# Attention's output halves added by a DMA within SBUF for three of four pairs of heads, and the epsilon term as a 65th column in the sum of the heads' squares

## The chip, the cores and the metric

The kernel runs on one core of a Trainium2 chip. The engines that matter are TensorE (PE, matrix products into PSUM), VectorE (DVE), ScalarE (ACT), GpSimd (POOL, which also issues DMAs on a queue of its own) and SyncE (SP, which only issues DMAs). Each engine takes its instructions in the order in which they are written into its queue. The metric is the device time of one execution in microseconds; runs of the kernel before gave a median of 1258.99 us.

## What is computed

One decoder layer on a sequence of 1024 tokens, width 1024. The part that matters here is attention: 8 heads of width 64, handled as four pairs, with an RMSNorm of each head of q and k, and stick-breaking weights in place of a softmax.

```python
def rms_norm(x, g):
    xf = x.astype(jnp.float32)
    y = xf * lax.rsqrt(jnp.mean(xf * xf, axis=-1, keepdims=True) + EPS)
    return (y * g.astype(jnp.float32)).astype(x.dtype)
...
    hn = rms_norm(h, norm1_g[i])
    proj = hn @ w_in[i]
    a_b, a_c, a_h, q, k, v, c_u, c_v = jnp.split(proj, split_idx, axis=-1)
    q = rms_norm(q.reshape(bsz, s_len, ATTN_HEADS, HEAD_DIM), q_norm_g[i])
    k = rms_norm(k.reshape(bsz, s_len, ATTN_HEADS, HEAD_DIM), k_norm_g[i])
    y_b = stick_breaking_attention(q, k, v).reshape(bsz, s_len, ATTN_W)
    h = h + jnp.concatenate([y_a, y_b, y_c], axis=-1) @ w_out[i]
...
        z = jnp.einsum('bqhd,bkhd->bhqk', qi, kj) * scale
        log_rem = jnp.where(causal, jax.nn.log_sigmoid(-z), 0.0)
        suffix = lax.cumsum(log_rem, axis=3, reverse=True) - log_rem
        weights = jnp.where(causal, jnp.exp(jax.nn.log_sigmoid(z) + suffix), 0.0)
        o = jnp.einsum('bhqk,bkhd->bqhd', weights, vj)
```

Convolution, spatial gating, the output projection, the squared-ReLU MLP and a gated input embedding complete the layer; the change does not touch them.

## The kernel before

Products are taken in three passes of parts: each float32 operand is split into a high part, rounded by ACT, and a low part, the difference, made by DVE or POOL (`split`).

`project(pr)` computes q, k and v of one pair of heads for eight blocks of 128 tokens. For each block PE accumulates a bank `qkv_ps` of 128x384. ACT squares the q and k columns into `qk_sq` (128 tokens by four head vectors of 64), DVE sums each 64 (L337), DVE scales the sums by 1/64 and adds an epsilon term that depends on the token (`ms1e[t]`, L339), POOL raises them to the power -1/2 (`rs`), and DVE multiplies q and k by that (`qk`, L345). `turn_qk` transposes the result on PE.

`attend(pr)` has eight steps, (head of the pair, group g of 256 query tokens). `stick` makes the weights: PE computes `z`, ACT two sigmoids (`rem`, `wt`), DVE a running product (the scan of L413), and DVE or POOL their product (L416). `gather` transposes the weights on PE (`w_tr`), splits them on ACT and DVE (`wT_hi`, `wT_lo`) and multiplies with V into `av`. V holds the high part of its 64 columns and the low part side by side, so rows 0 to 63 of `av` hold the one half of the output and rows 64 to 127 the other; they have to be added. That is L462 (ACT copies the lower rows to `av_lo`) and L463 (DVE adds them to the upper rows into `y_b`). `y_b` goes to `y_dram` by a DMA on SP, 128 rows for both heads of the pair, and is loaded again later for the output projection.

The order: `weave` interleaves attention of one pair with the projection of the next, or with the convolution for the last pair, by counts of matmul units. The tile framework then sets the order in each engine's queue by its own simulated timeline, and gives buffers out from pools (`half`, three buffers; `slot`, 56). On POOL's queue, `block_sums` sends transfers of 1 MB that build sums of blocks of a later weight matrix (`w_sums`) beside attention.

Of the kernel before, what the change touches and what calls it, by code (L numbers as in the profile page):

```python
# [7 lines left out]
F32 = mybir.dt.float32  # L8
F32R = mybir.dt.float32r
AF = mybir.ActivationFunctionType  # L10
ALU = mybir.AluOpType
AX = mybir.AxisListType

P = 128
# [4 lines left out]
HD = 64  # L19
# [13 lines left out]
def hybrid_block(ctx: ExitStack, tc: tile.TileContext, a: dict):  # L33
# [5 lines left out]
    nc = tc.nc  # L39
# [9 lines left out]
    tp = front.enter_context(tc.tile_pool(name="tp", bufs=6))  # L49
# [7 lines left out]
    def name(s):  # L57
        n_of[0] += 1
        return f"{s}_{n_of[0]}"

    def slot(s, dt=F32, shape=(P, HT)):
        return sp.tile(list(shape), dt, tag="slot", name=name(s))
# [10 lines left out]
    def halves(s, dt=F32, shape=(P, HT)):  # L73
        return [slot(s, dt, shape) for _ in range(2)]
# [1 line left out]
    def tmp(s, dt=F32, shape=(P, HT)):  # L76
        return tp.tile(list(shape), dt, tag="tmp", name=name(s))

    def half_tmp(s, dt=F32):
        return tp.tile([P, 256], dt, tag="half", name=name(s), bufs=3)  # L80

    def bank(pool, s):
        return pool.tile([P, HT], F32, tag=pool.name, name=name(s))
# [9 lines left out]
    half = [slice(0, HT), slice(HT, T)]  # L93
# [116 lines left out]
    ms1e, r1, r1h = [], [], []  # L210
# [89 lines left out]
                    nc.gpsimd.dma_start(w_sums[to, rows], src[rows])  # L300

    last_pool = [None]
    heads = {}
    y_dram = dram.tile([6, 2, P, HT], F32, name="y_dram")

    def project(pr):

        wk = [load_w(a["w_qkv"][pr, k], 384, nc.gpsimd if pr and k % 2 == 0 else nc.vector)
              for k in range(KT)]

        QS = [[None, None], [None, None]]

        KH = [[None, None], [None, None]]
        KL = [[None, None], [None, None]]
        V = [None] * 4
        low_q = [None, None]
        heads[pr] = QS, KH, KL, V, low_q
        for t in range(KT):
            th, ts = block(t)
            if t % 4 == 0:  # L320
                for hh, other in enumerate((hi_p, lo_p)):
                    KL[hh][th] = slot("KL", F32R)
                    nc.gpsimd.memset(KL[hh][th][other].bitcast(F32), 0.0)
                KH[0][th] = slot("KH", F32R)
                QS[0][th] = slot("QS", F32R)
                low_q[th] = slot("q_lo", F32R)
                QS[1][th] = slot("QS", F32R)
                KH[1][th] = slot("KH", F32R)
            ps = bank(ps_mm, "qkv_ps")[:, :384]
            for k0 in range(0, KT, 2):  # L330
                product(ps, [(cols(xn[k][th], ts), wk[k]) for k in (k0, k0 + 1)],
                        k0 == 0, k0 == KT - 2)
                yield 18
            sq = half_tmp("qk_sq")
            nc.scalar.activation(sq, ps[:, :256], AF.Square)
            ss = small.tile([P, 4], F32, tag="ss", name=name("ss"))
            nc.vector.tensor_reduce(out=ss, in_=sq.rearrange("p (h d) -> p h d", d=HD),  # L337
                                    axis=AX.X, op=ALU.add)
            nc.vector.tensor_scalar(out=ss, in0=ss, scalar1=1.0 / HD, scalar2=ms1e[t],  # L339
                                    op0=ALU.mult, op1=ALU.add)  # L340
            rs = small.tile([P, 4], F32, tag="rs", name=name("rs"))
            power_mhalf(rs, ss, 4)
            if t % 2 == 0:
                qk = tp.tile([P, 2, 256], F32, tag="qk", name=name("qk"), bufs=2)
            nc.vector.tensor_tensor(  # L345
                out=qk[:, t % 2].rearrange("p (h d) -> p h d", d=HD),
                in0=ps[:, :256].rearrange("p (h d) -> p h d", d=HD),
                in1=rs.unsqueeze(2).broadcast_to([P, 4, HD]), op=ALU.mult)
            if t % 2 == 0:
                V[t // 2] = slot("V", F32R, (P, 2, 2, 2, HD))  # L350
            v = V[t // 2][:, t % 2]
            split(ps[:, 256:].rearrange("p (h d) -> p h d", d=HD), v[:, :, 0], v[:, :, 1], scale=r1[t])
            if t % 2 == 1:
                later(72, lambda t=t, qk=qk: turn_qk(heads[pr], t, qk))
# [29 lines left out]
    def attend(pr):  # L384

        QS, KH, KL, V, _ = heads[pr]
        yb = halves("y_b")
        weights = {}

        def stick(hh, g):  # L390
            weights[hh, g] = []
# [31 lines left out]
        def gather(hh, g):  # L423
            own = slice(hh * HD, (hh + 1) * HD)
            wts = weights.pop((hh, g))
            av_of[0] ^= 1
            av = av_bank[:, av_of[0] * 256:(av_of[0] + 1) * 256]
# [17 lines left out]
            for j in range(-2, g + 1):  # L445
# [6 lines left out]
                for kb, o, first in parts:  # L452
                    m = 256 - first * P
                    lhs = V[kb // 2][:, kb % 2, hh].rearrange("p two d -> p (two d)")
                    for part in (hi, lo):
# [2 lines left out]
                                         stop=kb == 2 * g + 1 and part is lo)  # L458
                yield 8

            low = half_tmp("av_lo")
            nc.scalar.copy(low[:HD], av[HD:])  # L462
            nc.vector.tensor_tensor(out=yb[g // 2][own, (g % 2) * 256:(g % 2 + 1) * 256],  # L463
                                    in0=av[:HD], in1=low[:HD], op=ALU.add)
# [2 lines left out]

        steps = [(0, g) for g in range(4)] + [(1, g) for g in reversed(range(4))]
        yield from stick(*steps[0])
        for i, step in enumerate(steps):  # L470
            if i + 1 < len(steps):
                yield from stick(*steps[i + 1])
            block_sums(8 * pr + i, last_pool[0])
            yield from gather(*step)

    ATTEND = 2 * (72 + 8 * 10 + 72 + 10 * 10 + 80)

# [131 lines left out]
    for n in range(KT):  # L609
# [5 lines left out]
        for h in range(2):  # L615
            ps = wide_bank("pp_ps")
# [48 lines left out]
    ps = ctx.enter_context(tc.tile_pool(name="ps", bufs=8, space=PSUM, reuse_waits="tile"))  # L665
# [431 lines left out]
```

## Time and profile before

| | |
|---|---|
| median of 3 runs (lowest to highest) | 1258.99 us (1256.04 to 1264.21) |
| profiled execution | 1262.6 us |
| its span | 1260.9 us |
| PE busy in the span | 1215.0 us |
| DVE busy | 880.7 us |
| ACT busy | 603.8 us |
| POOL busy | 364.2 us |
| attention beside projections | 111 to 341 us of the span |

Times of lines and windows are microseconds from the start of the span; L12 is line 12 of the kernel. In the chain of waits each piece is followed back to what released it, so a piece of DVE in it is a moment at which all the rest waited for DVE. A busy PE is not PE at its peak, since matmuls are pipelined. The granted clock is the share of TensorE's full clock that was let through.

### The profile page before, as it was taken

What the parts mean: (1) busy time and instruction counts of PE and PEld (TensorE: products, weight loads), DVE (VectorE), ACT (ScalarE), POOL (GpSimd) and SP (SyncE); (2) the same over time, 40 slices, a digit from 0 to 9 for tenths busy, and PEclk for the clock granted to TensorE, in tenths of its full rate; (3) what the DMA queues carried; (4) which work ended last, traced back from release to release, by engine and by line L of the source; (5) the groups of instructions that cost most, each with busy time, mean ns of one, the idle gap of its engine ahead of it and who ended that gap; (6) DMA issues with size and microseconds to landing.
All of it is one profiled execution on the core that took longest, in us unless ns stands there. A gap on an engine that the chain in (4) does not pass through costs nothing.

```text
span 1260.9 us, 17509 instructions
## 1 busy us (share of the span) xinstructions
PE 1215.0 (96%) x5868; PEld 1034.1 (82%) x5868; DVE 880.7 (70%) x1324; ACT 603.8 (48%) x1167; POOL 364.2 (29%) x365
## 2 busy tenths in 40 slices
PE   9999898899999999879999999999999999999998
PEld 7898798898888878658888888888888888888887
DVE  7746886898979654676887777777755565686443
ACT  7725655666656454553334334344544344555211
POOL 2324434455323212233553453431000000122110
PEclk9999998999999999989999999999999999999999
DMA  9603257788542298689999999958956565653231
GB/s 309 211 18 117 84 158 210 167 210 159 119 114 38 67 292 226 175 221 251 269 244 255 252 244 250 252 193 302 354 179 224 183 223 170 203 166 106 76 111 51
DMA packets 118700, 234.89 MB, mean 186 GB/s; under 512 B 13105, under 2 KB 20529, under 8 KB 118353
## 3 DMA queue, kind: packets, MB, share of 16 engines
q1 hardware_dynamic: 94752, 168.08, 40.4%
q0 software_dynamic: 23856, 65.70, 23.3%
q8 instruction: 46, 0.75, 0.3%
q14 instruction: 46, 0.37, 0.1%
HBM read 176.57 MB, written 78.64 MB: 202 GB/s over the span
## 4 chain that ended last, share of the span: by engine, by line
PE 82%; DVE 8%; DMA 5%; issue 2%; ACT 1%; POOL 1%; SPq 0%; DVEq 0%; POOLq 0%; ACTq 0%
PE d_ps L731 24%; PE f_ps L731 24%; PE qkv_ps L161 3%; PE qkv_ps L162 3%; PE qkv_ps L163 3%; PE g_ps L161 2%; PE g_ps L163 2%; PE g_ps L162 2%; DVE rem L413 2%; PE av L456 2%; DMA S<-sq 2%; PE w_tr L438 1%; PE cv_ps L161 1%; DMA h_dram<-h 1%; PE cv_ps L162 1%
## 5 line engine op out<-in xcount | busy, mean ns | idle before, releaser
L135 DVE TENSOR_TENSOR w_lo<-raw,w_hi 128x512 fp32r<-128x512 f32 x268 | 244.9, 916 | 94.4 <-ACT w_hi L134 92.2
L134 ACT CAST w_hi<-raw 128x512 fp32r<-128x512 f32 x268 | 165.2, 619 | 242.6 <-PE d_ps L731 116.7
L731 PE MATMUL f_ps<-hn_hi,w_hi 128*128 128x512 f32 x448 | 176.5, 394 | 5.3 <-ACT v L884 5.3
L731 PE MATMUL f_ps<-hn_lo,w_hi 128*128 128x512 f32 x448 | 175.7, 392 | 0.0
L731 PE MATMUL f_ps<-hn_hi,w_lo 128*128 128x512 f32 x448 | 175.3, 392 | 0.0
L731 PE MATMUL d_ps<-f_hi,w_lo 128*128 128x512 f32 x448 | 174.3, 389 | 0.0
L731 PE MATMUL d_ps<-f_hi,w_hi 128*128 128x512 f32 x448 | 174.3, 389 | 0.0
L731 PE MATMUL d_ps<-f_lo,w_hi 128*128 128x512 f32 x448 | 174.3, 389 | 0.0
L731 PEld LDWEIGHTS f_ps<-hn_hi,w_hi 128*128 128x128 f32 x448 | 85.1, 190 | 23.4 <-ACT v L884 5.7
L719 POOL TENSOR_TENSOR S<-S,sq 128x512 f32<-128x512 f32 x14 | 22.6, 1614 | 273.5 <-ACT sq L788 273.5
L731 PEld LDWEIGHTS f_ps<-hn_lo,w_hi 128*128 128x128 f32 x448 | 85.1, 190 | 17.9 <-issue 0.2
L731 PEld LDWEIGHTS f_ps<-hn_hi,w_lo 128*128 128x128 f32 x448 | 85.0, 190 | 18.0
L731 PEld LDWEIGHTS d_ps<-f_hi,w_hi 128*128 128x128 f32 x448 | 84.1, 188 | 17.6
L731 PEld LDWEIGHTS d_ps<-f_lo,w_hi 128*128 128x128 f32 x448 | 84.1, 188 | 17.4
L731 PEld LDWEIGHTS d_ps<-f_hi,w_lo 128*128 128x128 f32 x448 | 84.1, 188 | 17.3
L413 DVE TENSOR_TENSOR_SCAN rem<-rem 128x128 f32<-128x128 f32 (+3 forms) x64 | 89.0, 1393 | 11.1 <-ACT rem L409 10.6
L161 PE MATMUL qkv_ps<-whi,xn_hi 128*128 128x384 f32 x256 | 92.0, 359 | 2.6 <-DVE V L138 2.6
L163 PE MATMUL qkv_ps<-whi,xn_lo 128*128 128x384 f32 x256 | 89.8, 351 | 0.0
L162 PE MATMUL qkv_ps<-wlo,xn_hi 128*128 128x384 f32 x256 | 89.8, 351 | 0.0
L135 DVE TENSOR_TENSOR f_lo<-raw,f_hi 128x512 fp32r<-128x512 f32 x112 | 77.6, 723 | 4.6 <-ACT f_hi L134 4.0
L134 ACT CAST f_hi<-raw 128x512 fp32r<-128x512 f32 x112 | 67.0, 620 | 17.9 <-DMA raw<-f_dram 13.4
L416 POOL TENSOR_TENSOR wt<-wt,rem 128x127 f32<-128x127 f32 (+4 forms) x40 | 44.3, 1109 | 107.7 <-DVE rem L413 44.9
(219 smaller groups left out, 2665.7 us busy)
## 6 DMA issues: line engine op xcount, KB each, us to landing
raw<-in_w_ff SPq DMA_DIRECT2D x160, 256.0 KB, 4.1
raw<-f_dram SPq DMA_DIRECT2D x112, 256.0 KB, 4.8
raw<-w_sums SPq DMA_DIRECT2D x64, 256.0 KB, 3.7
f_dram<-f SPq DMA_DIRECT2D x48, 256.0 KB, 4.4
f_dram<-t SPq DMA_DIRECT2D x48, 256.0 KB, 3.9
w_sums<-in_w_ff POOLq DMA_DIRECT2D x8, 1024.0 KB, 11.7
w_sums<-w_sums POOLq DMA_DIRECT2D x8, 1024.0 KB, 12.4
raw<-in_w_ff POOLq DMA_DIRECT2D x32, 256.0 KB, 5.4
```

The costliest lines, as they stand in the source:

```text
L134: nc.scalar.copy(hi, src)
L135: low.tensor_tensor(out=lo, in0=src, in1=hi, op=ALU.subtract)
L161: nc.tensor.matmul(ps, lh, rh, start=first and i == 0, stop=False)
L162: nc.tensor.matmul(ps, lh, rl, start=False, stop=False)
L163: nc.tensor.matmul(ps, ll, rh, start=False, stop=last and i == len(terms) - 1)
L413: nc.vector.tensor_tensor_scan(out=back, data0=back, data1=back, initial=1.0, op0=ALU.mult, op1=ALU.bypass)
L416: done = (nc.vector if on_vector else nc.gpsimd).tensor_tensor(out=wt[:, :W - 1], in0=wt[:, :W - 1], in1=rem[:, 1:W], op=ALU.mult)
L438: nc.tensor.transpose(tr[:, n:n + P], wts[i][:, kb * P:(kb + 1) * P], ident)
L456: nc.tensor.matmul(av[:, first * P:], lhs, part[:, o:o + m], start=kb == 0 and part is hi, stop=kb == 2 * g + 1 and part is lo)
L719: return eng.tensor_tensor(out=out, in0=x, in1=y, op=ALU.add)
L731: nc.tensor.matmul(bank, l, r, start=first and k == 0 and i == 0, stop=k == len(b) - 1 and i == 2, skip_group_check=True)
```

## The change

For the pairs 0, 1 and 2, ACT now copies all 128 rows of `av` into a tile `y_both` of 128x512, two groups into one tile. When both are there, a DMA on POOL's queue adds rows 64 to 127 onto rows 0 to 63 within SBUF. The store of the 64 rows is put off: it is called after the next even step, or in the next pair's attention after its first `stick`. The DVE addition is gone for these pairs; pair 3 keeps `y_b`. In the projection, `qk_sq` gets 65 columns for each head: ACT writes the epsilon term into the 65th, scales the squares by 1/64 as it makes them, and the reduction of L337 sums 65 columns, so that L339 is gone for all 32 blocks.

```diff
-    def half_tmp(s, dt=F32):
-        return tp.tile([P, 256], dt, tag="half", name=name(s), bufs=3)
+    def half_tmp(s, shape=(P, 256)):
+        return tp.tile(list(shape), F32, tag="half", name=name(s), bufs=3)
...
     last_pool = [None]
+    later_stores = []
...
-            sq = half_tmp("qk_sq")
-            nc.scalar.activation(sq, ps[:, :256], AF.Square)
+
+            sq = half_tmp("qk_sq", (P, 4, HD + 1))
+            nc.scalar.copy(sq[:, :, HD], ms1e[t].broadcast_to([P, 4]))
+            nc.scalar.activation(sq[:, :, :HD], ps[:, :256].rearrange("p (h d) -> p h d", d=HD),
+                                 AF.Square, scale=HD ** -0.5)
             ss = small.tile([P, 4], F32, tag="ss", name=name("ss"))
-            nc.vector.tensor_reduce(out=ss, in_=sq.rearrange("p (h d) -> p h d", d=HD),
-                                    axis=AX.X, op=ALU.add)
-            nc.vector.tensor_scalar(out=ss, in0=ss, scalar1=1.0 / HD, scalar2=ms1e[t],
-                                    op0=ALU.mult, op1=ALU.add)
+            nc.vector.tensor_reduce(out=ss, in_=sq, axis=AX.X, op=ALU.add)
...
-        yb = halves("y_b")
-        weights = {}
+        yb = halves("y_b") if pr == 3 else None
+        weights, both, summed, seen_g = {}, [None], [], []
+
+        def store_rows():
+
+            while summed:
+                to, t = summed.pop(0)
+                nc.sync.dma_start(to, t[:HD])
...
+            if yb is None:
+                if both[0] is None:
+                    both[0] = slot("y_both")
+                t = both[0]
+                nc.scalar.copy(t[:, (g % 2) * 256:(g % 2 + 1) * 256], av)
+                if len(seen_g) % 2:
+                    nc.gpsimd.dma_start(t[:HD], t[HD:], accum_op=ALU.add)
+                    summed.append((y_dram[pr, g // 2, own], t))
+                    both[0] = None
+                seen_g.append(g)
+                return
             low = half_tmp("av_lo")
...
         yield from stick(*steps[0])
+        while later_stores:
+            later_stores.pop(0)()
         for i, step in enumerate(steps):
...
             yield from gather(*step)
+            if i % 2 == 0:
+                store_rows()
+        later_stores.append(store_rows)
```

The framework orders the queues anew. Three places show what moved; the lines of the changed kernel are its own (L338 the square, L337 the column, L341 the reduction, L472 the av copy, L474 the addition by DMA).

ACT before, in pair 0 beside the projection of pair 1: sigmoids of `z` and squares of two blocks.

```order
L335 ACTIVATE qk_sq_1597<-qkv_ps_1512 128x256
L409 ACTIVATE rem_1485<-z_1487 128x128
L410 ACTIVATE wt_1486<-z_1487 128x128
L409 ACTIVATE rem_1485<-z_1493 128x512
L410 ACTIVATE wt_1486<-z_1493 128x512
L137 ACTIVATE V_1509<-qkv_ps_1512,r_566 128x2x64
L409 ACTIVATE rem_1519<-z_1521 128x256
L410 ACTIVATE wt_1520<-z_1521 128x256
L335 ACTIVATE qk_sq_1695<-qkv_ps_1607 128x256
L409 ACTIVATE rem_1519<-z_1527 128x512
```

ACT now, at the square of the same second block and the one after it.

```order
L416 ACTIVATE rem_1516<-z_1524 128x512
L417 ACTIVATE wt_1517<-z_1524 128x512
L338 ACTIVATE qk_sq_1691<-qkv_ps_1603 128x4x64
L337 COPY qk_sq_1994<-ms_726 128x4
L416 ACTIVATE rem_1578<-z_1580 128x384
L417 ACTIVATE wt_1579<-z_1580 128x384
L416 ACTIVATE rem_1578<-z_1586 128x512
L417 ACTIVATE wt_1579<-z_1586 128x512
L338 ACTIVATE qk_sq_1788<-qkv_ps_1703 128x4x64
L134 CAST wT_hi_1636<-w_tr_1631 128x512
L134 CAST wT_hi_1651<-w_tr_1646 128x512
L337 COPY qk_sq_2102<-ms_726 128x4
```

The column of a block three further on is written right behind a square (`qk_sq_1994` behind `qk_sq_1691`): the pool has three buffers, and 1994 takes that of 1691, so this copy waits for DVE's reduction of 1691.

DVE before, in pair 0 beside the projection of pair 1: the addition into `y_b`, the reductions and the scaling of their sums.

```order
L463 TENSOR_TENSOR y_b_1345<-av_87,av_lo_1854 64x256
L379 COPY QS_1409<-q_lo_1410 64x512
L337 TENSOR_REDUCE ss_1922<-qk_sq_1920 128x4
L135 TENSOR_TENSOR wT_lo_1945<-w_tr_1939,wT_hi_1944 128x512
L135 TENSOR_TENSOR wT_lo_1960<-w_tr_1954,wT_hi_1959 128x512
L339 TENSOR_SCALAR ss_1922<-ss_1922,ms_726 128x4
L337 TENSOR_REDUCE ss_2001<-qk_sq_1999 128x4
L413 SCALAR_TENSOR_TENSOR rem_2019<-rem_2019 128x384
L413 SCALAR_TENSOR_TENSOR rem_2029<-rem_2029 128x512
L339 TENSOR_SCALAR ss_2001<-ss_2001,ms_726 128x4
L345 TENSOR_TENSOR qk_1927<-qkv_ps_1811,rs_1925 128x256
```

DVE now, at the same place (scan of 384 and of 512 columns).

```order
L423 TENSOR_TENSOR wt_1874<-wt_1874,rem_1873 128x767
L135 TENSOR_TENSOR wT_lo_1940<-w_tr_1934,wT_hi_1939 128x512
L135 TENSOR_TENSOR wT_lo_1955<-w_tr_1949,wT_hi_1954 128x512
L341 TENSOR_REDUCE ss_1997<-qk_sq_1994 128x4
L420 SCALAR_TENSOR_TENSOR rem_2014<-rem_2014 128x384
L420 SCALAR_TENSOR_TENSOR rem_2024<-rem_2024 128x512
L135 TENSOR_TENSOR wT_lo_1973<-w_tr_1968,wT_hi_1972 128x384
L346 TENSOR_TENSOR qk_1922<-qkv_ps_1927,rs_1999 128x256
```

The addition and both scalings are gone; the reduction stands alone, and POOL's `rs` follows it at once.

POOL before, at the first steps of pair 1: weight products, the 1 MB transfers and `rs`.

```order
L416 TENSOR_TENSOR wt_2339<-wt_2339,rem_2338 128x383
L300 DMA w_sums<-in_w_ff 16x16384 x2
L169 TENSOR_TENSOR rs_2379<-ss_2376,mhalf 128x4
L169 TENSOR_TENSOR rs_2476<-ss_2473,mhalf 128x4
L416 TENSOR_TENSOR wt_2401<-wt_2401,rem_2400 128x639
L300 DMA w_sums<-in_w_ff 16x16384 x2
L169 TENSOR_TENSOR rs_2586<-ss_2583,mhalf 128x4
```

POOL now, at the same place.

```order
L423 TENSOR_TENSOR wt_2329<-wt_2329,rem_2328 128x383
L300 DMA w_sums<-in_w_ff 16x16384 x2
L474 DMA y_both_2188<-y_both_2188 64x512
L169 TENSOR_TENSOR rs_2369<-ss_2367,mhalf 128x4
L169 TENSOR_TENSOR rs_2465<-ss_2463,mhalf 128x4
L423 TENSOR_TENSOR wt_2390<-wt_2390,rem_2389 128x639
L300 DMA w_sums<-in_w_ff 16x16384 x2
L474 DMA y_both_2387<-y_both_2387 64x512
L169 TENSOR_TENSOR rs_2574<-ss_2572,mhalf 128x4
```

Two additions stand right behind pairs of 1 MB transfers on the same queue, and ahead of `rs`.

## The prediction

> **What bounds the kernel now.** I read the page's first two parts, then the busy time by stage, then the chain that ended last in the stage that the change edits, and last the timelines of single engines there. The profiled execution took 1262.6 us, of which 1260.9 is the span. The table of stages has the columns us, PE, PEld, DVE, ACT, POOL (each busy us and instructions), granted PE clock, DMA share and GB/s.
>
> ```profile
> core 0: us, PE busy (x) PEld busy (x) DVE busy (x) ACT busy (x) POOL busy (x), PEclk, DMA share, GB/s
> 57.00:111.00 54.00, 53.90 (x309) 50.41 (x308) 26.26 (x77) 18.80 (x43) 15.28 (x18) 1.00 0.06 23
> 111.00:170.00 59.00, 51.67 (x307) 48.37 (x306) 47.58 (x73) 36.12 (x85) 26.64 (x25) 0.94 0.33 116
> 170.00:230.00 60.00, 54.53 (x327) 51.91 (x325) 44.28 (x82) 35.06 (x85) 27.70 (x31) 0.91 0.65 194
> 230.00:290.00 60.00, 53.78 (x340) 50.59 (x340) 54.82 (x93) 38.16 (x94) 31.91 (x32) 0.97 0.89 205
> 290.00:341.00 51.00, 46.60 (x309) 43.98 (x308) 45.63 (x75) 35.19 (x83) 19.38 (x18) 1.00 0.64 120
> 560.00:860.00 300.00, 300.00 (x1318) 247.94 (x1318) 231.14 (x267) 117.65 (x201) 129.62 (x118) 1.00 0.90 248
> ```
>
> From 560 us on, PE is full, so what is won earlier reaches the end. From 57 to 111 PE is full as well (53.90 of 54): the first pair's projection, which runs there, gains nothing from less DVE work. Attention beside the next pair's projection, 111 to 341 us, is different: PE is busy 206.6 of 230 us and idles 23.4, and DVE is busy 192.3. The chain says who is late there.
>
> ```profile
> by line: PE qkv_ps L161 11.7%; DVE rem L413 11.2%; PE qkv_ps L162 10.9%; PE qkv_ps L163 10.8%; PE av L456 6.2%; issue 5.3%; DVE wT_lo L135 4.6%; PE w_tr L438 4.2%; DMA stage<-in_w_qkv 3.7%; DVE ss L339 2.8%; DVE wt L416 2.5%; DVE KL L370 2.
> 131.15 0.43 DVE y_b L463
> 155.28 1.03 DVE ss L339
> 176.68 0.77 DVE ss L339
> 189.96 8.72 DMA stage<-in_w_qkv
> ...
> 272.26 1.98 DVE ss L339
> 317.80 0.32 DVE y_b L463
> ```
>
> This is the window 111 to 346 us. Scans (L413) are the largest DVE share and stay. Two operations that the change takes off DVE are in the chain themselves: L339 with 2.8% of 235 us, 6.6 us, and L463 with twelve pieces, the first and last shown, that add up to 4.4 us.
>
> **The change, part by part.** First the operations in that window, by form, and why L339 costs what it does.
>
> ```profile
> L339 DVE TENSOR_SCALAR ss<-ss,ms 128x4 f32<-128x4 f32 x26 | 11.0, 427 | 0.3
> L463 DVE TENSOR_TENSOR y_b<-av,av_lo 64x256 f32<-64x256 f32 x22 | 9.0, 411 | 1.5 <-ACT av_lo L462 1.2
> L339 DVE TENSOR_SCALAR ss<-ss,ms x32: 203/229/1984, 82.3 to 345.6; 128x4 f32<-128x4 f32 x32
> L337 DVE TENSOR_REDUCE ss<-qk_sq x32: 399/419/421, 81.9 to 343.7; 128x4 f32<-128x256 f32 x32
> 152.02 0.40 DVE L337 TENSOR_REDUCE ss<-qk_sq 128x4 f32<-128x256 f32 x1
> ...
> 272.26 1.98 DVE L339 TENSOR_SCALAR ss<-ss,ms 128x4 f32<-128x4 f32 x1
> 272.24 1.97 POOL L135 TENSOR_TENSOR wlo<-stage,whi 128x384 fp32r<-128x384 f32 x2
> ```
>
> L339 has four columns and a median of 229 ns, but up to 1984 ns. The last two rows, of the engines' timelines, show why: the long one started 0.02 us after POOL's wlo products and ended 0.03 us after them (272.24 + 1.97 = 274.21 against 274.24). It waited for POOL in its own slot. The reduction L337 never does (399 to 421 ns). So 26 L339 take 11.0 us of DVE in the window, about 5 of them standing. They go; the reduction gets 260 columns for 256, four columns more of 419 ns: nothing that counts.
>
> Of the 32 L463 the 24 of the first three pairs go, 22 of them by this window's count. DVE loses 20.0 (11.0 + 9.0) of its 192 us. On the chain that is 6.6 + 4.4 = 11.0 us. Not all of it arrives: the load of 8.72 us at 189.96 is followed by ACT and PE, and its landing is not set by DVE. I take what lies ahead of it as swallowed there: L463 at 131, 151 and 171 us (0.43 + 0.41 + 0.43) and L339 at 155 and 176 us (1.03 + 0.77), 3.1 us. That leaves 7.9. If the load moves forward with the rest, it is 11.0; if scans take every place freed, it is 0.
>
> What is added lands on ACT, POOL, SP and the DMA queues.
>
> ```profile
> L335 ACT ACTIVATE qk_sq<-qkv_ps 128x256 f32<-128x256 f32 x26 | 9.9, 384 | 6.2 <-PE qkv_ps L163 5.8
> L462 ACT COPY av_lo<-av 64x256 f32<-64x256 f32 x22 | 8.1, 370 | 6.8 <-PE av L456 6.4
> L410 ACT ACTIVATE wt<-z 128x128 f32<-128x128 f32 x11 | 3.2, 292 | 6.4 <-PE w_tr L438 6.4
> L790 POOL DMA_DIRECT2D S<-sq x14 | 12.0, 860 | 19.7 <-ACT sq L788 9.8 <-DMA S<-sq 8.2 <-DMA raw<-in_xT 0.7
> L300 POOL DMA_DIRECT2D w_sums<-in_w_ff x16 | 8.7, 547 | 0.0
> L297 POOL DMA_DIRECT2D w_sums<-w_sums x7 | 8.1, 1438 | 0.1
> ```
>
> ACT, av: a copy of 128x256 takes the place of one of 64x256. L335 reads 128x256 in 384 ns, L462 370: 14 ns each, 0.3 us for 24, which hides like the next. PE's next av group then waits for ACT alone and no longer for DVE behind it.
>
> ACT, the column: 26 copies of 128x4 in the window. No row has it; the nearest, 128x128, takes 292 ns, which is the upper end; the lower is 0, where it fits in an idle gap. I take 0.25 us, 6.5 us of ACT. ACT is busy 144.5 of the 230 us, so this alone hides.
>
> ACT, the wait: this is the part with teeth. The column copy of tile n+3 writes the buffer whose reduction on DVE has to be over, and the order puts it right behind the square of tile n: of 29 such copies 13 have none or one ACT row in between, five of them before attention, where ACT is idle most of the time (18.80 of 54 us busy), and eight in the window. ACT stands there until DVE has reduced, and behind it stand the w_tr and z evictions that feed DVE and PE. How late is the reduction? A short and a long case:
>
> ```profile
> 126.61 0.38 ACT L335 ACTIVATE qk_sq<-qkv_ps 128x256 f32<-128x256 f32 x1 [0.72 <-PE qkv_ps L163]
> 127.03 0.42 DVE L337 TENSOR_REDUCE ss<-qk_sq 128x4 f32<-128x256 f32 x1 [2.04 <-ACT qk_sq L335]
> 253.27 0.39 ACT L335 ACTIVATE qk_sq<-qkv_ps 128x256 f32<-128x256 f32 x1
> 256.14 0.41 DVE L337 TENSOR_REDUCE ss<-qk_sq 128x4 f32<-128x256 f32 x1
> ```
>
> From the end of the square to the end of the reduction 0.46 and 2.89 us; the mean over 16 pairs that I could match in the timelines is 1.07. Eight copies standing 1.07 less 0.25 of work in between make 6.6 us of ACT; the others, with two to six rows between, wait only on long backlogs like the second case, and I put them at 3.4 in all: 10 us. Since ACT idles more than a third of the window and part of this falls into its gaps, I charge a quarter, 2.5 us. The ends are 0 and 27.8 us (26 copies, 1.07 each, all on the path).
>
> POOL: twelve DMA issues. Nearest in kind is L790, an addition by DMA into SBUF, 860 ns; the ends are 547 (L300) and 1438 (L297). Twelve make 10.3 us (6.6 to 17.3) on an engine busy 105.6 of 230 us. Each also waits for ACT's av copy, with rs and wt products queued behind it. POOL is in the chain for only a few pieces, so I charge 0.5 us.
>
> SP: twelve stores replace six, each 0.33 us of issue, on a queue that mostly waits: 0. They wait for the additions to land; behind them stand w_qkv and w_conv loads, and slots of y_both are reused by memsets on POOL and copies on ACT. That is a rival, below.
>
> Clock: rows of 6 us where DVE is full and PE short.
>
> ```profile
> 154.00:160.00 6.00, 3.91 (x15) 3.67 (x16) 5.90 (x9) 1.75 (x5) 2.77 (x2) 0.72 0.00 0
> 232.00:238.00 6.00, 3.25 (x19) 2.50 (x20) 5.92 (x10) 4.30 (x10) 2.81 (x3) 1.00 1.13 208
> 238.00:244.00 6.00, 6.00 (x30) 6.00 (x29) 4.81 (x5) 0.40 (x2) 2.98 (x1) 0.72 1.13 208
> ```
>
> A PE gap is followed by a granted clock of 0.72, which costs 0.28 x 6 = 1.7 us. The clock of the three stages from 111 to 290 us (0.94, 0.91, 0.97) holds 0.06 x 59 + 0.09 x 60 + 0.03 x 60 = 10.7 us of this. I count one such slice as saved, 1.7, because the gap before the first row holds a long L339.
>
> Sum: -7.9 + 2.5 + 0.5 - 1.7 = -6.6 us, 1256.0 against the profiled 1262.6. That execution lies 3.6 above the median of the three runs shown (1258.99), so the forecast is 1252.4, given as 1252.
>
> **The rivals.** *A, more is won.* All 11.0 us arrive and five slices at 0.72 go (8.5 us): 19.5, so 1239.5 on the median's scale. For it: qk waits for the rs that waits for L339, and the 3.9 us from the end of the reduction at 152.42 to that of its L339 at 156.31 shrink to nothing. Against: scans stay and fill DVE. The Trainium skill (TensorE: Matmul & The Clock Gate, What's actually happening) states that the clock falls after an idle window of about 3.4 us. By that rule these shorter gaps would cost no clock, and A would give 11.0 us only, 1248; the trace's 0.72 rows disagree, and I keep the row.
>
> *B, slower: ACT stands behind DVE.* If three quarters of the 27.8 us reach the path, 20.9 less 7.9 makes 13.0 us more, 1272; all of it makes 1279. Three quarters is the point from which it decides. For it: DVE has backlogs of 2 to 3 us, in which the reduction waits behind scans. Against: ACT's slack, 85 us.
>
> *C, the additions land late and give the gain back.*
>
> ```profile
> w_sums<-w_sums POOLq DMA_DIRECT2D x7, 1024.0 KB, 14.4
> y_dram<-y_b SPq DMA_DIRECT2D x5, 256.0 KB, 8.0
> ```
>
> Five of the twelve additions stand right behind a pair of 1 MB transfers on the same queue. At 14.4 us to land, and 8.0 for the store, a slot comes free 22 us after the issue; a step of attention takes about 230/24 = 9.6. At the places where a memset or an av copy wants that slot, an engine stops; two such stops of 3 to 4 us give 1259. The Trainium skill (SBUF — State Buffer, Door 1 and its section on the setup cost) says that 64 partitions reach 8 of the 16 ports, 196 GB/s measured. By that alone the 128 KB land in some 2.7 us, an estimate from that page with its 2 us fixed cost, and C would be void; I hold with the queue's row.
>
> *D, nothing arrives*: scans fill every freed place, 1259.
>
> **How the numbers follow.** Forecast 0.45 (1247 to 1258), A 0.20, C 0.15, D 0.10, B 0.10. The likeliest gives 1252. The range 1240 to 1268 takes in most of A and half of B's 27.8 us (13.9 - 7.9 = 6.0, 1265), with POOL at its upper end (17.3 us) for the rest; outside stay the rest of B and a little of A. A change of under 1%, 12.6 us, is about what a measurement of this kernel can tell from none: faster 0.20 (A), slower 0.10 (B), within 0.70.
>
> **What would show it.** DVE in the attention stage down by some 20 us, no TENSOR_SCALAR beside the reduction, and y_b in the last pair alone; PE idle below 23 us. Right for the ACT term: waits of ACT's 128x4 copy on the reduction add to 10 us or less. Wrong: those waits add to 20 or more with w_tr evictions late; or POOL memsets and y_both copies wait for the stores; or the DVE time falls and PE's idle time does not. A change after 443 us, where the order only shifts by a few rows, would be outside this account.

## The result and the profile after

The changed kernel takes 1240.82 us (median of four runs, 1238.52 to 1243.24) against 1261.42 us of the kernel before, measured beside it: a ratio of 0.9846, with an interval of 0.9821 to 0.9871. It is 1.3 to 1.8% faster, where the forecast was 1252. The profiled execution has a span of 1241.5 us, 19.4 less than before. Of all runs behind the ratios below one was slow, 1713.93 us for the column with L339's work aside, and no ratio counts it.

Two stages, the projections of the pairs with attention beside them (from the first to the last `qkv_ps` product) and the output projection (`o_ps`), hold most of it. Columns as in the table of stages above; first the changed kernel, then the one before.

```profile
75.10:324.10 249.00, 236.67 (x1479) 226.49 (x1478) 195.51 (x313) 159.96 (x406) 120.81 (x126) 0.97 0.63 158
426.60:522.10 95.50, 94.03 (x406) 76.42 (x406) 55.16 (x88) 52.91 (x92) 23.01 (x31) 0.98 0.85 244
```

```profile
76.20:339.60 263.40, 239.88 (x1479) 227.69 (x1478) 208.34 (x365) 157.19 (x374) 115.95 (x116) 0.96 0.56 143
443.40:543.10 99.70, 96.34 (x405) 77.00 (x406) 53.87 (x86) 51.64 (x90) 24.04 (x32) 0.97 0.82 226
```

The first stage is 14.4 us shorter: TensorE idles 12.3 us for 23.5, which is 11.2, and the same 1479 recorded products take 3.2 us less. About half of that is the clock: it was granted at one half for 20.5 us of the stage before and for 17.1 us now, and half of the difference is 1.7 us. The output projection is 4.2 shorter. The stretch ahead of the first stage gives 1.1, the convolution's end 1.3, the tail 0.4; the next 320 us give 2.0 back, and the last two large stages do not change.

What TensorE waited for in the first stage (us, times, the longest), changed kernel first:

```profile
PE w_tr L445 <- DVE KL L371: 3.8, 3, 1.7
PE w_tr L445 <- DVE wt L423: 2.5, 3, 1.4
PE av L463 <- DVE wT_lo L135: 2.0, 4, 0.8
...
PE z L409 <- ACT wt L417: 1.4, 5, 0.4
PE av L463 <- ACT y_both L472: 0.5, 2, 0.3
```

```profile
PE qk_tr L364 <- DVE qk L345: 5.6, 4, 2.7
PE av L456 <- DVE wT_lo L135: 4.0, 4, 1.7
...
PE av L456 <- DVE y_b L463: 2.6, 4, 1.3
PE w_tr L438 <- DVE wT_lo L135: 2.2, 1, 2.2
```

The largest wait of before, for `qk`, is gone altogether; that for y_b became 0.5 us for ScalarE's copy; those for `wT_lo` fell as well, and 1.4 us for `wt` came in. The largest single part of it is time lost on the way of a block of q and k from its product to `qk` and the transposition. That way has its steps on four engines: product (TensorE), square (ScalarE), reduction and, before the change, L339 (VectorE), rs (POOL), qk (VectorE). It is what the experiments below turn on, so here it is from the trace of each kernel. Each block has eight L163 products; the first column is the time from the end of the eighth to the start of the block's square, the second from the square's end to the end of the block's `qk` (means over the 26 or 27 blocks whose square starts after 105 us).

```
kernel                     product to square   square to qk   first qkv_ps to first o_ps
before                           2.02 us          5.89 us            367.2 us
before, second execution         2.04             5.98               368.3
changed                          0.49             4.40               351.6
changed, second execution        0.50             4.46               350.5
```

The second part lost L339's step. The first lost 1.5 us a block, although the change does nothing at that place. One block of the kernel before shows how: its product ended at 199.37 + 0.34 = 199.71, and ScalarE squared it at 204.28. Timelines of ScalarE, VectorE and POOL (start, us, what):

```profile
203.89 0.37 ACT L462 COPY av_lo<-av 64x256 f32<-64x256 f32 x1
204.28 0.38 ACT L335 ACTIVATE qk_sq<-qkv_ps 128x256 f32<-128x256 f32 x1
```

```profile
205.89 0.42 DVE L463 TENSOR_TENSOR y_b<-av,av_lo 64x256 f32<-64x256 f32 x1
206.34 0.42 DVE L337 TENSOR_REDUCE ss<-qk_sq 128x4 f32<-128x256 f32 x1
206.67 0.48 DVE L138 SCALAR_TENSOR_TENSOR q_lo<-qk_tr,c_gq,QS 128x256 fp32r<-128x256 f32 x1
207.07 0.22 DVE L339 TENSOR_SCALAR ss<-ss,ms 128x4 f32<-128x4 f32 x1
```

```profile
207.37 1.04 POOL L169 TENSOR_TENSOR rs<-ss,mhalf 128x4 f32<-128x4 f32 x1 [2.84 <-DVE ss L339]
```

The square stands directly behind an `av_lo` copy, and its reduction behind that copy's y_b addition. Squares and `av_lo` come from one pool of three buffers, `half`, and the framework sets the order with it. In the order of the kernel before, 15 of the 32 squares stand directly behind an `av_lo` copy; in the changed one, whose first three pairs take no `av_lo`, 3 of 32 stand directly behind an `av_lo` or `y_both` copy. No wait in the trace of the kernel before is put down to that pool, so if it costs time, it does so through the order.

### The profile page after: what moved, and what is told of

The parts are those of the page before. It is cut to its first block, busy times and chain, and to the rows that moved or that the text cites. A ratio compares the mean times of both kernels' runs of the same rounds, so it can differ in the third digit from the quotient of the medians.

```text
span 1241.5 us, 17505 instructions
## 1 busy us (share of the span) xinstructions
PE 1207.3 (97%) x5868; PEld 1029.7 (83%) x5868; DVE 871.1 (70%) x1268; ACT 604.5 (49%) x1199; POOL 369.0 (30%) x377
## 4 chain that ended last, share of the span: by engine, by line
PE 83%; DVE 6%; DMA 5%; issue 3%; ACT 2%; POOL 1%; SPq 0%; POOLq 0%; ACTq 0%; DVEq 0%
PE d_ps L754 25%; PE f_ps L754 24%; PE qkv_ps L161 3%; PE qkv_ps L162 2%; PE qkv_ps L163 2%; PE g_ps L161 2%; PE g_ps L163 2%; PE g_ps L162 2%; DVE rem L420 2%; PE av L463 2%; DMA y_both<-y_both 2%; PE w_tr L445 2%; PE o_ps L161 2%; PE o_ps L163 2%; PE o_ps L162 2%
## 5 line engine op out<-in xcount | busy, mean ns | idle before, releaser
L420 DVE TENSOR_TENSOR_SCAN rem<-rem 128x128 f32<-128x128 f32 (+3 forms) x64 | 92.2, 1446 | 18.7 <-ACT rem L416 17.6
L163 PE MATMUL qkv_ps<-whi,xn_lo 128*128 128x384 f32 x256 | 89.1, 348 | 0.0
L423 POOL TENSOR_TENSOR wt<-wt,rem 128x127 f32<-128x127 f32 (+4 forms) x40 | 47.1, 1194 | 82.5 <-DVE rem L420 39.9
```

The source lines that it names most:

```text
L163: nc.tensor.matmul(ps, ll, rh, start=False, stop=last and i == len(terms) - 1)
L420: nc.vector.tensor_tensor_scan(out=back, data0=back, data1=back, initial=1.0, op0=ALU.mult, op1=ALU.bypass)
L423: done = (nc.vector if on_vector else nc.gpsimd).tensor_tensor(out=wt[:, :W - 1], in0=wt[:, :W - 1], in1=rem[:, 1:W], op=ALU.mult)
```

## The experiments

Eighteen runs were made, two of them of the unaltered kernels, each in five rounds with the kernel before on the same chip. Ratios are to it; 0.01 is 12.6 us. Three theories stand at the start. W: VectorE's work is what is won, as the prediction reckoned. Q: the way from the reduction to `qk`, which L339 lengthened (as P, with the square at its start, it comes back below). O: any shift of the framework's order would win.

**One part alone.** The column without the addition by DMA, the addition without the column, and L339 as an activation of ScalarE:

```diff
-            nc.vector.tensor_scalar(out=ss, in0=ss, scalar1=1.0 / HD, scalar2=ms1e[t],
-                                    op0=ALU.mult, op1=ALU.add)
+            nc.scalar.activation(ss, ss, AF.Identity, scale=1.0 / HD, bias=ms1e[t])
```

> The kernel before with the 65th column alone; the row halves are still added on VectorE. Theory W (VectorE's work in the attention stage is what is won, each piece of it alike): of the 19.4 us the column gives the part of L339 in the work removed, 11.0 of 20.0, so about -10.7 us (-8 to -13). Theory Q (what is won is the path from the reduction to rs to qk, which L339 lengthened by its own backlog): -15 or more. Theory O (the scheduler's order, which shifts everywhere with any edit, makes the difference): this run and the next don't add up to -19.4 within 6 us, or one of them is slower than before.

> The kernel before with the addition by DMA alone; L339 stays. Theory W: 9.0 of 20.0 of the work, about -8.7 us (-6 to -11). Theory Q: -4.4 us at most, the chain's share of L463. Theory O: does not add up with the run of the column to -19.4 within 6 us.

> The kernel before with L339 as an Identity activation on ScalarE (scale 1/64, bias the mean term) in place of the operation on VectorE: VectorE loses the same work as by the column, but the path to rs keeps a step and gains a change of engine. Theory W: about -10 us, like the column. Theory Q: 0 to +6 us, since ScalarE's queue takes the place of VectorE's. Theory O: anything within 10 us of before.

The column: 1247.3 us, 0.9900 (0.9874 to 0.9925). The addition: 1247.25, 0.9911 (0.9885 to 0.9937). L339 on ScalarE: 1247.4, 0.9899 (0.9879 to 0.9919). Each alone wins 11 to 13 us, and the two of the change together not the sum of some 24 but 19 to 20: they overlap. W comes nearest to these three. Q as it was put fails: it had 15 us or more for the column, at most 4.4 for the addition and no gain for L339 on ScalarE. O is not excluded, since three different edits won the same.

**Work added.** L339 in two operations in the kernel before; and in the changed kernel one of its form beside the way, for nobody:

```diff
+            aside = small.tile([P, 4], F32, tag="aside", name=name("aside"))
+            nc.vector.tensor_scalar(out=aside, in0=ss, scalar1=1.0 / HD, scalar2=ms1e[t],
+                                    op0=ALU.mult, op1=ALU.add)
```

> The kernel before with L339 split in two TENSOR_SCALARs, one for the factor and one for the mean term: 32 more operations on VectorE, nothing taken away. So far three edits that each took some work off VectorE won 11 to 13 us each. Theory W (the work itself): slower than before by 7 us (32 x 0.23, the median of L339) to 13 us (32 x 0.40, its mean). Theory O (the order before is an unlucky one, and any edit that shifts it wins): faster than before by 5 us or more.

> The changed kernel with a TENSOR_SCALAR of L339's form behind each reduction that writes a tile nobody reads: VectorE gets the work back, the path from the reduction to rs stays without it, and the order of the engines is nearly that of the changed kernel. Theory W: 8 to 13 us slower than the changed kernel. Theory Q (the path alone): within 2 us of it.

Two operations on the way: 1268.59 us, 1.0061 (1.0039 to 1.0083), slower by 5 to 10 us; so not every shift of the order wins. The same operation aside: 1238.96, 0.9833 (0.9812 to 0.9854), where the changed kernel has 0.9846 in its own group and 0.9848 below. VectorE got 32 operations back, and nothing was lost. W falls in the changed kernel, as far as L339's work goes. The same was then done to the kernel with the column alone, where VectorE still adds the halves:

> The kernel before with the 65th column, and behind each reduction a TENSOR_SCALAR of L339's form that writes a tile nobody reads: the path from the reduction to rs is short, VectorE's work is that of before or a little more, and the y_b additions stay. Theory P (the path from square to qk is what the column wins): 11 to 13 us faster than before, like the column alone. Theory W (VectorE's work): within 2 us of before. Since VectorE has less slack here than in the changed kernel, where the same operation cost nothing, a mixture would lie between, at 4 to 9 us faster.

1245.14 us, 0.9886 (0.9863 to 0.9909): all of the column's gain with all of the work. The operation was there, and as long as before, here and in the run above (duration min, median, max in ns; first and last start):

```profile
L341 DVE TENSOR_SCALAR aside<-ss,ms x32: 194/220/2304, 82.0 to 334.0; 128x4 f32<-128x4 f32 x32
```

```profile
L343 DVE TENSOR_SCALAR aside<-ss,ms x32: 201/228/1611, 81.7 to 327.1; 128x4 f32<-128x4 f32 x32
```

Its longest ones are as long as those of L339, which stood beside POOL's products. So the column does not win by work taken off VectorE. What it takes away on the way is L339's step between the reduction and rs: over the blocks after 105 us 1.30 us passed on average from the end of the reduction to the end of L339, for an operation with a median of 0.23; and a second such step cost 5 to 10 us. But the length of the step does not price the gain: with L339 on ScalarE (the third run above) 0.96 us of it were still there, and that kernel won as much as the column. What it won there stays open, and so does whether work added aside would cost something in the kernel before itself, which was not run.

**What the addition by DMA wins.** First the bank's hand-back: ScalarE copies both halves, VectorE still adds.

```diff
+            up = half_tmp("av_up")
+            nc.scalar.copy(up[:HD], av[:HD])
...
-                                    in0=av[:HD], in1=low[:HD], op=ALU.add)
+                                    in0=up[:HD], in1=low[:HD], op=ALU.add)
```

> The kernel before with both row halves copied out by ScalarE and added on VectorE from there: TensorE gets its bank back from ScalarE, as with the addition by DMA, but VectorE keeps its 32 additions and ScalarE gets 32 copies more. Theory W: VectorE's work is unchanged, so no gain, 0 to +3 us against before. Theory H (the bank's hand-back is what the addition by DMA wins): faster than before by 5 us or more.

1257.52 us, 0.9977 (0.9963 to 0.9991): 1 to 5 us, not 11. The new copies `av_up` take buffers of `half` too, so this run frees the bank and burdens the pool. Then VectorE's 24 additions put back into the changed kernel:

> The changed kernel with 24 additions on VectorE of L463's size put back, from the copy in SBUF into a tile nobody reads: VectorE gets 24 x 0.41 = 10 us of work back, nobody waits for it, and TensorE's bank goes back to ScalarE as in the change. Theory W: 8 to 11 us slower than the changed kernel. Theory S (VectorE has slack in the changed kernel, and work that nobody waits for costs nothing there): within 3 us of it.

1248.25 us, 0.9913 (0.9893 to 0.9934), which looks like W. But the sentence that nobody waits for them was wrong. They read `y_both`, so the addition by DMA had to wait until they were done, and they took buffers of `half` again:

```profile
POOL y_both L477 <- DVE aside L473: 15.6, 6, 5.0
```

In that run the squares start 3.2 us behind their product, for 0.5 in the changed kernel. So once more, reading a tile that VectorE wrote itself and writing a buffer of their own:

> The changed kernel with 24 additions on VectorE of L463's size, this time from a tile that VectorE wrote itself, into a tile nobody reads, so that no engine waits for them (in the run before this one the POOL queue did, 15.6 us). Theory W (the addition won by VectorE's work): 6 to 10 us slower than the changed kernel, ratio to before 0.990 to 0.993. Theory S (work that nobody waits for costs nothing; the addition won by the waits behind it): within 3 us of the changed kernel, ratio 0.982 to 0.987.

1241.89 us, 0.9852 (0.9831 to 0.9874): nothing lost. All 24 ran, at the length of L463, and no engine waited for one:

```profile
L475 DVE TENSOR_TENSOR aside<-wT_lo x24: 390/413/978, 125.0 to 337.2; 64x256 f32<-64x256 f32 x24
```

W falls here too, in the changed kernel. What is left of what the addition changed is the pool. One line of the kernel before, nothing else:

```diff
-            low = half_tmp("av_lo")
+            low = tp.tile([P, 256], F32, tag="av_lo", name=name("av_lo"), bufs=1)
```

> The kernel before with a buffer of its own for av_lo, so that it no longer shares the three with the squares. The addition by DMA took av_lo of three pairs out of that pool as well. If the sharing was the cost: 5 to 11 us faster than before. If not: within 3 us of before, or what the order alone makes of it.

1243.25 us, 0.9862 (0.9840 to 0.9885). This buffer alone, with every operation of before, wins 17 us (14 to 20), nearly all of the change's gain and more than the 5 to 11 expected. Only 5 of the 32 squares still stand directly behind an `av_lo` copy, and the block shown above now has its square ahead of that copy, 0.04 us after its product (196.46 + 0.34 = 196.80):

```profile
196.46 0.34 PE L163 MATMUL qkv_ps<-whi,xn_lo 128*128 128x384 f32 x1
```

```profile
196.84 0.38 ACT L335 ACTIVATE qk_sq<-qkv_ps 128x256 f32<-128x256 f32 x1 [0.16 <-PE qkv_ps L163]
197.16 0.47 ACT L137 ACTIVATE QS<-qk_tr,c_gq 128x256 fp32r<-128x256 f32 x1
197.66 0.37 ACT L462 COPY av_lo<-av 64x256 f32<-64x256 f32 x1
```

The way in all kernels, in the order of the time from the first `qkv_ps` to the first `o_ps`:

```
kernel                          product to square   square to qk   first qkv_ps to first o_ps
changed, no additions by DMA          0.30 us          4.07 us           342.0 us
changed, four buffers                 0.43             4.33              346.3
changed, column late                  0.68             4.28              346.9
changed, 24 additions aside           0.46             4.52              347.4
changed, L339's work aside            0.53             4.47              349.7
changed                               0.49             4.40              351.6
column and own buffer                 0.37             4.42              351.8
changed, additions by DMA later       0.52             4.53              353.5
column alone                          2.68             4.38              353.6
addition by DMA alone                 0.51             5.32              354.4
changed, 24 additions from y_both     3.21             4.56              354.4
own buffer alone                      0.32             5.25              354.7
column, L339's work aside             1.98             4.43              355.1
L339 on ScalarE                       2.19             5.40              356.5
column late and own buffer            0.49             4.45              357.2
bank handed back by ScalarE           1.91             5.76              365.1
before                                2.02             5.89              367.2
L339 in two operations                1.87             6.92              373.9
```

(Five rows belong to runs told below.) Where `av_lo`, or an addition put aside, draws on the squares' pool in all four pairs, the squares start 1.9 to 3.2 us behind the product; where that is so in the last pair alone or not at all, 0.3 to 0.7. The last three kernels, 365 to 374 us, are those in which both parts are long: 1.9 us or more and 5.8 or more. In the other fifteen, 342 to 357 us, one of the two is short, the first at most 0.7 or the second at most 5.4. To shorten one part went with most of the gain, which fits that the gains overlap. But the line was drawn after the runs, it runs between 5.40 and 5.76, and the sum of the two columns does not order the kernels: 7.8 us with 354.4 stands against 7.7 with 365.1.

One rival is left: a fourth buffer in the shared pool of the kernel before was not tried, so the runs do not tell the sharing from a pool that is too small for both.

**Both causes removed without a DMA.** The column and the own buffer, VectorE adding as before; and the same with the column written from the projection's bank.

> The kernel before with the 65th column and a buffer of its own for av_lo; the additions stay on VectorE and no DMA adds. Theory R (what is won is the time from the product's end to qk: the square freed from av_lo's buffers, and L339 off the way to rs): square 0.3 to 0.6 us behind the product, qk 4.4 to 4.6 behind the square, and 18 to 25 us faster than before, as fast as the changed kernel or faster. Theory H (TensorE's bank handed back by ScalarE and 24 additions off VectorE count on their own): 4 us or more slower than the changed kernel, ratio above 0.988.

> The same with the column written from the projection's bank, so that ScalarE doesn't wait for an earlier reduction. Theory R: like the run beside it, 1 to 3 us faster at most.

1243.53 us, 0.9877 (0.9856 to 0.9898), and 1248.23, 0.9918 (0.9896 to 0.9941). The way is as short as in the changed kernel, yet the kernel is no faster than with the own buffer alone, and its 0.9877 lies below the 0.988 that was set for theory H and short of the 18 us that were set for R; for the second run R had 1 to 3 us faster than the first, and it was slower. So the way tells the fast kernels from the slow ones, but does not order the fast ones, and some 4 us of the changed kernel's lead over the first run stay without a cause, as far as they are clear of noise. The two runs beside each other differ by 4.7 us for a column written in another manner, which moves the order of all engines: differences of this size between kernels of different order I put down to no cause.

**The wait that the column brings.** Four buffers for the squares, and the column tied behind the product:

```diff
-            nc.scalar.copy(sq[:, :, HD], ms1e[t].broadcast_to([P, 4]))
+            nc.scalar.activation(sq[:, :, HD], ps[:, :4], AF.Identity, scale=0.0, bias=ms1e[t])
```

> The changed kernel with four buffers for the squares in place of three, the order of the engines kept. The column copies waited 11.2 us in all on the reduction. If a quarter of that was on the path, as predicted: 1.5 to 4 us faster than the changed kernel. If ScalarE's idle time took it all: within 1.5 us of it. If all was on the path: 8 to 11 us faster.

> The changed kernel with the column written from the projection's bank by an Identity activation of factor 0 and bias ms: it can't be put ahead of the product any more, so it stands right in front of the square and no longer waits for an earlier reduction (11.2 us of waits in the changed kernel). If a quarter of those waits was on the path: 2 to 4 us faster than the changed kernel. If ScalarE's idle time took them: within 1.5 us. If the 0.2 us ahead of each square count on the path to qk instead: 3 to 6 us slower.

Four buffers: 1236.99 us, 0.9818 (0.9799 to 0.9836), but the waits stayed (11.5 us in 15 places), since the framework moved each copy ahead by one block more; the run tells nothing of them. The late column: 1237.99, 0.9837 (0.9813 to 0.9861). There the waits on a reduction are gone, and the time is that of the changed kernel within the interval: 1.4 us less by the ratios, at most some 6 with both intervals, which is what those waits can be worth.

**What the additions by DMA cost.** Left out; and tied behind the next step's product on POOL:

> The changed kernel with the twelve additions by DMA left out: only the upper rows of each block go on to the output, and the halves of three pairs of heads are not summed. If the additions cost what the prediction put down (0.5 us on POOL, the one wait of 1.2 us for a store on top): 0 to 2 us faster than the changed kernel. If late landings hold the stage (rival C): 4 us or more faster.

> The changed kernel with each addition by DMA tied behind the last product on POOL of the following step, so that POOL does not stand for ScalarE's copy (9.9 us in three places); the other engines keep their order nearly. If these stands cost what leaving the additions out won (about 4 to 6 us): 2 to 5 us faster than the changed kernel. If POOL's slack takes them: within 1.5 us of it. If the later landings hold slots: slower by 2 us or more.

Left out: 1234.68 us, 0.9796 (0.9775 to 0.9816), against the changed kernel's 0.9846 and 0.9848 some 6 us faster, 2 to 10 with both intervals. That is the 4 us or more that had been set for rival C, but the order of TensorE shifts with it, so part may be that. Later: 1241.51, 0.9862 (0.9839 to 0.9885), no gain. Here the landings were shorter, a median of 3.3 us for 7.5, but POOL still stood 10.0 us in three places for ScalarE's copy, for 9.9 in the changed kernel, so this run does not tell what that wait costs. What the additions cost, and by what, stays open.

**The two kernels once more.**

> The changed kernel unaltered, on the chip of the three runs beside it and with their runs of before: 1236 to 1243 us, ratio to before 0.982 to 0.987; it gives the comparisons of this group their reference and shows how far the stages differ between two executions of one kernel.

> The kernel before unaltered: 1256 to 1265 us. Its profile shows how far the stages of one kernel differ between two executions, above all the 99.7 us of the stage of the output projection and the granted clock of the three attention stages, 0.94, 0.91 and 0.97. If the clock there is chance, it differs by 0.03 or more; if it follows TensorE's gaps, it repeats.

The changed kernel: 1240.33 us, 0.9848 (0.9824 to 0.9872). The one before: 1257.81, 0.9987 (0.9969 to 1.0005), the length of its first stage 265.1 us for 263.4, with 23.6 us of TensorE idle for 23.5. The granted clock from 111 to 290 us was 0.94, 0.94, 0.94 for 0.94, 0.91, 0.97. Two of these differ by the 0.03 that was set for chance. Yet the stretches at half clock begin near the same five places in both executions, at 118.6, 156.2, 180.1, 204.0 and 234.7 us for 118.7, 156.2, 180.1, 204.0 and 238.2; two of them differ in length, and one more came at 320 us. So the clock repeats in the main, and chance moves it by a stretch or two of 3.4 us. The output projection took 97.8 us before and 93.9 after, so its 4 us are there again. But over all kernels it ranges from 93.9 to 99.8 without following any edit: 95.9 with L339 doubled, 99.4 with the column alone, 99.8 with additions aside. Its cause stays open.

## Why the prediction was wrong

The direction was right, the size was not: 6.6 us less forecast, 19.4 less in the profiled spans (1252 against 1240.8 us).

- **The step that failed is the price of the operations removed**: so many pieces of L339 and L463 in the chain by their durations, 6.6 + 4.4 = 11.0 us, of which 7.9 were to arrive. Durations on VectorE were the wrong measure. The column alone, which removes L339, won 11 to 13 us, and L339's work put back aside cost nothing (0.9833 and 0.9886). L463's work put back aside cost nothing in the changed kernel either (0.9852). What counted was where the operations stood: L339 put 1.30 us between reduction and rs for each block, though how much of the gain this explains stays open, since the kernel with 0.96 us of it left, on ScalarE, won as much; and L463's partner `av_lo` stood ahead of the squares. In the changed kernel VectorE is busy 195.5 of 249 us.
- **What the account lacked** is the pool that `av_lo` shared with the squares. That `av_lo` leaves it stood in the diff, and that squares stand behind `av_lo` copies stood in the order and the timelines. The prediction costed the copies of `av` by their length only. This buffer alone won 17 us, and with it the squares start 0.32 us behind their product for 2.02.
- **The 3.1 us swallowed at the load of 8.72 us**: nothing shows that they were. In the changed kernel ScalarE's table of waits has no w_qkv load in this stage any more; before it had 6.0 us of them.
- **The clock, one slice, 1.7 us**, was right for this stage: half clock for 17.1 us in place of 20.5, which is 1.7 us. The same products took 3.2 us less there, and the rest of that is not explained. In the output projection half clock fell from 6.4 to 3.4 us, 1.5 us of the 2.3 that its products took less.
- **ScalarE's wait for the reduction** was sized well. 10 us of it were expected, a quarter on the path (from a mean of 1.07 us over 16 pairs; over all 27 blocks after 105 us it is 1.24); 11.2 are there,

```profile
L337 ACT COPY qk_sq<-ms x32: 182/198/283, 76.3 to 295.9; 128x4 f32<-128x4 f32 x32
...
  DVE ss L341: 11.2, 15
```

and without them the kernel is at most some 6 us faster. Rival B did not come. The copy takes 0.20 us, for 0.25 taken.
- **POOL, 0.5 us** for twelve issues at 0.86: the addition's line in the changed kernel has (min, median, max in ns; then us to landing)

```profile
L474 POOL DMA_DIRECT2D y_both<-y_both x12: 847/916/2083, 129.5 to 344.6; - x12
...
DMA to landing us min/median/max: 2.7/7.5/23.6
```

The median is 0.92 us, for 0.86 taken, but leaving them out won 2 to 10 us. This term was too small, or the order moved with them.
- **Rival C, late landings**: they came. The median was 7.5 us, the longest 23.6, behind transfers of 1 MB; the store that followed held ScalarE for 1.18 us, the only wait of ScalarE for such a store in this stage. Whether they cost more stays open: leaving the additions out won 2 to 10 us, shorter landings won nothing. Chain of waits, then ScalarE's timeline, changed kernel:

```profile
256.92 23.57 DMA y_both<-y_both
...
280.55 2.21 DMA y_dram<-y_both
```

```profile
282.87 0.37 ACT L137 ACTIVATE V<-qkv_ps,r 128x128 fp32r<-128x128 f32 x1 [1.18 <-DMA y_dram<-y_both]
```

The two additions with nothing ahead of them on the queue, issued at 129.5 and 344.6 us, landed in 2.7 us. That is the estimate that the prediction worked out from the Trainium skill (SBUF — State Buffer, Door 1 and its section on the setup cost); the trace agrees for these two, and the other ten took 2.9 to 23.6 us.
- **Rival A** gave 1239.5, and the time lies there, but as a sum of other terms: its 11.0 us of operations are not what was won, and of its five clock slices one went in the stage.
- **What was to be seen**: no TENSOR_SCALAR beside the reduction, y_b in the last pair alone, and TensorE's idle time well below 23 us all came. VectorE's busy time fell by 12.8 us from the first to the last `qkv_ps`, not by 20, and a gain after 443 us, outside the account, came with 4 us.

The range held the time at its lower end, because A had been counted in.

## What to carry to other kernels

In this kernel an operation taken off an engine was worth its place, not its duration. Follow the way on which it stands, from producer to consumer over all engines, and price the time between its neighbours' ends; put the same work back aside to see which of the two it was. And list, for each tile that a change takes out of a buffer pool, who else draws on that pool: here a pool shared by two chains went with an order that held one of them up, without any wait that the trace names, and one more buffer won most of what the rewrite won.

## What the runs showed of the hardware

TensorE's clock fell after short gaps. Two gaps in the changed kernel's first stage, one of them the longest there, in brackets behind the products that ended them, and the slices around or behind them:

```profile
150.85 0.57 PE L445 MATMUL w_tr<-ident,wt 128*128 128x128 f32 x3 [1.13 <-DVE KL L371]
269.53 0.44 PE L161 MATMUL qkv_ps<-whi,xn_hi 128*128 128x384 f32 x1 [1.77 <-DVE V L138]
```

```profile
150.00:156.00 6.00, 5.15 (x22) 5.16 (x23) 5.94 (x8) 1.81 (x5) 1.77 (x1) 0.72 0.00 0
270.00:276.00 6.00, 6.00 (x29) 5.87 (x29) 3.31 (x5) 2.49 (x9) 2.24 (x2) 0.72 1.13 207
```

Gaps of 1.13 and 1.77 us, each at the end of a stretch in which TensorE was busy only part of the time (2.42 of the 4.00 us from 146 us on, 2.58 of the 4.50 us from 265 us on), went with a slice at 0.72. A gap of 1.38 us that ended at 121.79 us did not: the six microseconds behind it have 1.00. So the length of the gap alone does not decide. The Trainium skill (TensorE: Matmul & The Clock Gate, What's actually happening) gives an idle window of about 3.4 us as what lowers the clock; no gap in this stage is that long, so as a rule on single gaps it does not hold here, and the measurement decides.

VectorE's TENSOR_SCALAR of four columns, with a median of 0.23 us, took up to 2.0 us where rs waited for it and up to 2.3 us where it was put aside. Aside, this standing cost nothing that the runs could measure (0.9833 for 0.9846, 0.9886 for 0.9900), with the reduction ahead of it and `qk` behind it on the same engine.
